# GLA cores of a hybrid encoder: split float32r products, float32r transposes and a moved query projection

## Chip, cores and metric

The kernel runs on one core of one Trainium2 chip. The metric is the device time of one execution in microseconds (us). A core has five engines with a queue each: PE (TensorE, matrix products and transposes; its weight loads are shown apart as PEld), DVE (VectorE), ACT (ScalarE), POOL (GpSimd) and SP, which here only issues DMAs. ACT and POOL issue DMAs too.

## What is computed

A two-layer encoder over 512 tokens of width 1024. Layer 0 mixes tokens by bidirectional gated linear attention (GLA), layer 1 by softmax attention; each is followed by a gated MLP with a width-3 convolution. The change lies in the GLA mixer alone, which in the reference is, cut to its core:

```python
GLA_HEADS, GLA_DK, GLA_DV, GLA_CHUNK = 4, 128, 256, 64
proj = h @ w_in                        # q, k, v, g, r
la_f = heads(log_sigmoid(r_f @ w_up_f + b_f) / 16)     # and la_b, backward

def gla_chunked(q, k, v, log_a, strict):
    b = cumsum(log_a, axis=3)          # within a chunk
    b_end = b[:, :, :, -1:, :]
    q_dec, k_inv = q * exp(b), k * exp(-b)
    att = where(mask, einsum('bhncd,bhnsd->bhncs', q_dec, k_inv), 0.0)
    o_intra = einsum('bhncs,bhnsv->bhncv', att, v)
    kv_chunk = einsum('bhncd,bhncv->bhndv', k * exp(b_end - b), v)
    # s_prev: scan over chunks, state = decay_chunk * state + kv_chunk
    o_inter = einsum('bhncd,bhndv->bhncv', q_dec, s_prev)
    return (o_intra + o_inter).reshape(B, H, S, dv)

o_f = gla_chunked(q, k, v, la_f, strict=False)
o_b = flip(gla_chunked(flip(q), flip(k), flip(v), flip(la_b), strict=True))
o = rmsnorm(o_f + o_b, norm_w) * silu(g)
return o @ w_out
```

## The kernel before

Activations lie transposed, features on partitions and tokens along the free dimension: `x` is eight tiles of 128 x 512. Most products are done in "split float32r": an operand is written as a high part, rounded to float32r by a copy on ACT, and a low part, the difference, by a subtraction on DVE. A product is then three float32r products, high x high, high x low and low x high (`mm3`, L347 to L351). Weights come by SP's DMAs in raw form and are split on ACT and DVE (`split`, L198 and L199) one or two pieces ahead of use, in three buffers.

The program is written as straight code; a planner then decides, with its own estimate of each operation's time, in which order each engine takes its instructions, the earlier one in the program first among those that it thinks ready. The estimate fixes the order only: on the chip each engine waits for what its next instruction needs. Tiles come from tagged pools with a fixed number of buffers; the PSUM banks are "acc" (3), "s" (2), "pt" (2) and "po" (1), and the SBUF tags of concern are "t" (6), "u" (4), "g" (22, made by `big`), "xhl" (8) and "ring" (1). `tc.issue_after(ins)` ties instructions behind another one on the same engine.

The GLA (`gla`, from L426) first projects values `v` and gates `g` for all heads, with the decays of all heads and both directions beside them (`gate`: `EK[h, d]` holds the two exponentials, 512 columns for queries and 512 for keys, `FK[h, d]` the decays of super-chunks of 128 tokens). Then come the four heads. Each has

- `proj(h)`: 24 products for the keys (psk) and 24 for the queries (psq), each multiplied by the token norm on DVE (L550, L553) into `kqt`. Head h+1 is projected in the program before head h's core.
- `core(h)`: for each direction DVE multiplies the key exponential by the keys and the query exponential by the queries, in place (L561, L562), and POOL makes the keys weighted to the end of the super-chunk (`ends`, L565). PE transposes these in float32 (kt, L572), ACT copies them out (kts, L574). PE makes inner products of keys and queries in float32 (in, L584); ACT copies the forward ones (`at`, L586), DVE puts the backward ones over them above the diagonal (L589). PE makes keys times v in float32 (kv, L607), ACT and DVE sum these to the states (L608, L610), in PE's order three for each direction; the third goes to bank "po". Then the last head's tail, then the outputs (L631): for each of four groups of 128 tokens `at` times v and up to two products with states, all float32. Squares on ACT (L635), a reciprocal root on POOL (L283), and the scaling by the gates on DVE into `g` (L638).
- `tail(h)`: PE transposes the gated outputs in float32 (tp, L644), ACT and DVE split them (L646, L647) into a tile of tag "xhl" each for the out-projection.

Beside head 0, ACT takes the gates' silu and POOL multiplies them by the norm weights (L653). After head 3, twelve steps of the out-projection (op, L406) run before head 3's tail.

Of the kernel before, what the change touches and what calls it, by code (L numbers as in the profile page):

```python
# [20 lines left out]
GH, DK, DV = 4, 128, 256  # L21
# [33 lines left out]
def hybrid_encoder_kernel(  # L55
# [30 lines left out]
    def nm(s):  # L86
        uid[0] += 1
        return f"{s}{uid[0]}"
# [15 lines left out]
    def tiny(w, n, tag="tiny"):  # L104
        return sp.tile([P, 8], F32, tag=tag, bufs={"tiny": 36, "tiny2": 4}[tag], name=nm(n))[:, :w]
# [141 lines left out]
    for c in range(KC):  # L247
        r = slice((c % 4) * S, (c % 4 + 1) * S)
# [26 lines left out]
    def rsqrt_eps(src, w, n, scale=None, tag="tiny"):  # L275

        t = tiny(w, n, tag)
        if scale is None:
            dve.tensor_scalar(t, src, EPS, None, ALU.add)
        else:  # L280
            dve.tensor_scalar(t, src, scale, EPS, ALU.mult, ALU.add)
        r = tiny(w, n, tag)
        pool.tensor_tensor(r, t, halfneg[:, :w], ALU.pow)  # L283
        return r
# [62 lines left out]
    def mm3(ps, wh, wl, mh, ml, start, stop):  # L347

        mm(ps, wh, mh, start=start, stop=False)  # L349
        mm(ps, wh, ml, start=False, stop=False)  # L350
        mm(ps, wl, mh, start=False, stop=stop)  # L351

    def feature_steps(wh, wl, hl, ps):

# [71 lines left out]
    def gla(norm, nxt):  # L426
# [115 lines left out]

        oh = [None] * KC

        def proj(h):
            kqt = big(F32, "kq")
            tag = "acc" if h else "pt"
            psk = bank(tag, "k")
            feature_tile(*W.half(w_kq, 2 * h), norm.hl, psk)
            dve.tensor_tensor(kqt[:, S:], psk, norm.R, ALU.mult)  # L550
            psq = bank(tag, "q")
            feature_tile(*W.half(w_kq, 2 * h + 1), norm.hl, psq)
            dve.scalar_tensor_tensor(kqt[:, :S], psq, DK ** -0.5, norm.R, ALU.mult, ALU.mult)  # L553
            return kqt

        def core(h, kqt, then):
            ends = big(F32, "end")
            ends = [ends[:, :S], ends[:, S:]]
            for d in range(2):
                e, f = EK[h, d], ends[d]  # L560
                dve.tensor_tensor(e[:, S:], e[:, S:], kqt[:, S:], ALU.mult)  # L561
                dve.tensor_tensor(e[:, :S], e[:, :S], kqt[:, :S], ALU.mult)  # L562
                sup = slice(0, 3) if d == 0 else slice(1, 4)
                v3 = lambda t: t.rearrange("p (s t) -> p s t", t=P)[:, sup, :]
                pool.tensor_tensor(v3(f), v3(e[:, S:]), FK[h, d][:, sup].rearrange("p (s o) -> p s o", o=1)  # L565
                                   .to_broadcast([P, 3, P]), ALU.mult)

            orders, keys = ([0, 1, 2], [3, 2, 1]), []
            for d, order in enumerate(orders):
                kt = bank("pt", "kt")  # L570
                for i, s in enumerate(order):
                    pe.transpose(kt[:, i * P : (i + 1) * P], ends[d][:, s * P : (s + 1) * P], ident)  # L572
                kts = tmp("t", "kts")
                act.activation(kts[:, : 3 * P], kt[:, : 3 * P], AF.Copy)  # L574
                keys.append(kts)

            at = tmp("t", "at")
            banks = []
            for d in range(2):
                e = EK[h, d]  # L580
                b = bank("acc" if h == GH - 1 else "s", "in")
                for s in range(NT):
                    o = s * P
                    mm(b[:, o : o + P], e[:, S + o : S + o + P], e[:, o : o + P], start=True, stop=True)  # L584
                banks.append(b)
            act.activation(at, banks[0], AF.Copy)  # L586

            def upper():
                dve.copy_predicated(at3, msk, banks[1].rearrange("p (s c) -> p s c", c=P))  # L589

            at3 = at.rearrange("p (s c) -> p s c", c=P)
            msk = smask.rearrange("p (o c) -> p o c", o=1).to_broadcast([P, NT, P])

            st = {}
            hs = slice(h * DV, (h + 1) * DV)
            for d, order in enumerate(orders):
                kts = keys[d]
                sa = tmp("t", "sa")
                sb = tmp("t", "sb") if d == 0 else st["b"]
                st["b"] = sb  # L600
                step = 1 if d == 0 else -1
                kv = bank("acc", "kv")
                kv2 = bank("po", "kv2")
                place = [kv[:, :DV], kv[:, DV:], kv2[:, :DV]]
                slot = [sa[:, :DV], sa[:, DV:], sb[:, d * DV : (d + 1) * DV]]
                for i, s in enumerate(order):
                    mm(place[i], kts[:, i * P : (i + 1) * P], v[s][:, hs], start=True, stop=True)  # L607
                act.activation(slot[0], place[0], AF.Copy)  # L608
                for i in (1, 2):
                    last = dve.scalar_tensor_tensor(slot[i], slot[i - 1], FK[h, d][:, order[i] : order[i] + 1],  # L610
                                                    place[i], ALU.mult, ALU.add)
                for i, s in enumerate(order):
                    st[d, s + step] = slot[i]
                if d == 0:
                    with tc.issue_after(last.ins) if h == GH - 1 else ExitStack():
                        upper()
            if then is not None:
                then()

            oss = tiny(4, "oss")  # L620
            og = []
            for s in range(NT):
                if s % 2 == 0:
                    bo = bank("s", "o")
                po = bo[:, (s % 2) * DV : (s % 2 + 1) * DV]
                parts = [(at[:, s * P : (s + 1) * P], v[s][:, hs])]
                for d in range(2):
                    if (d, s) in st:
                        parts.append((EK[h, d][:, s * P : (s + 1) * P], st[d, s]))
                for i, (l, r) in enumerate(parts):  # L630
                    mm(po, l, r, start=i == 0, stop=i == len(parts) - 1)  # L631
                og.append(po)
            for s in range(NT):
                junk = tmp("sq", "junk", DV)
                act.activation(junk, og[s], AF.Square, accum_out=oss[:, s : s + 1])  # L635
            ors = rsqrt_eps(oss, NT, "ors", 1.0 / DV)
            for s in range(NT):
                dve.scalar_tensor_tensor(g[s][:, hs], og[s], ors[:, s : s + 1], g[s][:, hs], ALU.mult, ALU.mult)  # L638

        def tail(h):  # L640
            for c in (2 * h, 2 * h + 1):
                tp = bank("pt", "tp")
                for s in range(NT):
                    pe.transpose(tp[:, s * P : (s + 1) * P], g[s][:, c * P : (c + 1) * P], ident)  # L644
# [3 lines left out]
                oh[c] = (t[:, :S], t[:, S:])  # L648

        kqt = proj(0)  # L650
        for j in range(NT):
            act.activation(g[j], g[j], AF.Silu)
            pool.tensor_tensor(g[j].rearrange("p (h c) -> p h c", c=DV), g[j].rearrange("p (h c) -> p h c", c=DV),  # L653
                               gnw.rearrange("p (o c) -> p o c", o=1).to_broadcast([P, GH, DV]), ALU.mult)
# [495 lines left out]
```

## Time and profile before

| | us |
|---|---|
| median of three runs | 1116.74 |
| the three runs | 1116.59, 1116.74, 1118.1 |
| the profiled execution | 1117.63 |
| its span, first to last instruction | 1115.9 |
| PE busy in it | 1110.2 |
| DVE, ACT, POOL busy | 792.9, 550.3, 120.6 |

The granted clock of PE was 1.0 in the whole execution. Times within the profile count from the span's start; a row of a timeline has the start, the length, the engine, the line of the kernel, the operation, the tile written, the tiles read, the shape and how many instructions are merged, and in brackets how long the engine had been idle and what released it. Matrix products overlap in PE's pipeline, so that the length of one (0.39 us for 512 columns) is more than the distance to the next; the chain of waits gives the distances.

### The profile page before, as it was taken

The page shows a single profiled execution, that of the slowest core. Times are in us where ns is not written, and L with a number is a line of the kernel's source. Part 1 is how long each engine was busy: PE and PEld are TensorE (multiplying, and loading weights), DVE is VectorE, ACT ScalarE, POOL GpSimd, SP SyncE. Part 2 cuts the span into 40 slices and gives each one's busy share as a digit, 9 for nine tenths or more (in the row PEclk, how much of TensorE's full clock was granted, in tenths as well). Part 3 has the DMA queues.
Part 4 walks back from the last instruction along what each step waited for, and adds up shares of the span by engine and source line. Part 5 has one row for each costly group of instructions (what it writes and reads, how often), then busy time and mean ns, then how long its engine had stood idle before and what let it go on. Part 6 is the DMA issues. An engine that isn't in the chain of part 4 may idle for free.

```text
span 1115.9 us, 14785 instructions
## 1 busy us (share of the span) xinstructions
PE 1110.2 (99%) x5836; PEld 953.7 (85%) x5836; DVE 792.9 (71%) x1221; ACT 550.3 (49%) x818; POOL 120.6 (11%) x114
## 2 busy tenths in 40 slices
PE   9999999999999999999999999999999999999998
PEld 7888888888889988898888888888888998889887
DVE  6786654577789677975755688756778957797572
ACT  5565233444556444553464667644454644465340
POOL 0104110000101000100004343000010100010000
PEclk9999999999999999999999999999999999999999
DMA  6322220223226523363247765422222652336322
GB/s 234 144 83 76 76 76 25 90 78 111 76 76 171 156 90 113 95 157 125 97 118 186 192 174 161 140 88 85 104 76 76 171 165 80 113 95 170 115 76 76
DMA packets 30790, 128.57 MB, mean 115 GB/s; under 512 B 3584, under 2 KB 4224, under 8 KB 20352
## 3 DMA queue, kind: packets, MB, share of 16 engines
q1 hardware_dynamic: 21216, 102.30, 26.8%
q0 software_dynamic: 4608, 16.78, 7.9%
q10 hardware_dynamic: 4896, 8.54, 2.0%
q8 instruction: 46, 0.75, 0.3%
q14 instruction: 24, 0.20, 0.1%
HBM read 100.34 MB, written 2.10 MB: 92 GB/s over the span
## 4 chain that ended last, share of the span: by engine, by line
PE 98%; DVE 1%; DMA 0%; issue 0%; ACT 0%; ACTq 0%; SPq 0%; DVEq 0%
PE r L754 14%; PE up L349 14%; PE up L350 14%; PE up L351 14%; PE op L406 8%; PE vg L380 8%; PE dn L351 2%; PE dn L350 2%; PE dn L349 2%; PE o L631 2%; PE av L380 1%; PE kv L607 1%; PE A L349 1%; PE A L350 1%; PE A L351 1%; PE pt L1009 1%
## 5 line engine op out<-in xcount | busy, mean ns | idle before, releaser
L349 PE MATMUL up<-xhl,wh 128*128 128x512 f32 x704 | 274.4, 390 | 0.0
L350 PE MATMUL up<-xhl,wh 128*128 128x512 f32 x704 | 274.0, 389 | 0.0
L351 PE MATMUL up<-xhl,wl 128*128 128x512 f32 x704 | 273.9, 389 | 0.0
L198 ACT ACTIVATE wh<-raw 128x1024 fp32r<-128x1024 f32 x132 | 139.5, 1057 | 227.3 <-PE up L350 108.4
L199 DVE TENSOR_TENSOR wl<-raw,wh 128x1024 fp32r<-128x1024 f32 x132 | 164.3, 1245 | 40.2 <-ACT wh L198 40.0
L351 PEld LDWEIGHTS up<-xhl,wl 128*128 128x128 f32 x704 | 132.1, 188 | 27.8
L349 PEld LDWEIGHTS up<-xhl,wh 128*128 128x128 f32 x704 | 132.2, 188 | 27.0
L350 PEld LDWEIGHTS up<-xhl,wh 128*128 128x128 f32 x704 | 132.2, 188 | 27.0
L754 PE MATMUL r<-gu,wh 128*128 128x256 f32 x640 | 116.3, 282 | 0.0
L754 PEld LDWEIGHTS r<-gu,wh 128*128 128x128 f32 x640 | 99.7, 191 | 0.3
L696 DVE TENSOR_TENSOR u<-up,R 128x512 f32<-128x512 f32 x88 | 60.1, 685 | 54.4 <-PE up L351 54.4
L754 PE MATMUL r<-gu,wl 128*128 128x256 f32 x320 | 90.4, 283 | 0.0
L698 ACT ACTIVATE y<-u,cw 128x512 f32<-128x512 f32 x88 | 71.2, 811 | 33.0 <-DVE u L696 32.8
L380 PE MATMUL vg<-wh,xhl 128*128 128x512 f32 x256 | 80.1, 391 | 0.4 <-DVE wh L196 0.4
L406 PE MATMUL op<-oT,wh 128*128 128x512 f32 x256 | 71.8, 394 | 0.0
L700 DVE SCALAR_TENSOR_TENSOR y<-u,cw,y 128x511 f32<-128x511 f32 x88 | 65.7, 748 | 2.0
L699 DVE SCALAR_TENSOR_TENSOR y<-u,cw,y 128x511 f32<-128x511 f32 x88 | 65.4, 744 | 1.2 <-ACT y L698 1.2
L702 ACT ACTIVATE y<-y 128x512 f32<-128x512 f32 x44 | 27.8, 632 | 72.0 <-DVE y L700 71.8
L754 PEld LDWEIGHTS r<-gu,wl 128*128 128x128 f32 x320 | 61.1, 191 | 0.0
L188 POOL DMA_DIRECT2D wl<-raw x32 | 28.3, 884 | 292.7 <-ACT wl L141 140.8
L380 PEld LDWEIGHTS vg<-wh,xhl 128*128 128x128 f32 x256 | 48.1, 189 | 10.9 <-ACT sq L323 0.6
L406 PEld LDWEIGHTS op<-oT,wh 128*128 128x128 f32 x256 | 47.2, 188 | 9.5 <-ACT oT L646 0.3
(221 smaller groups left out, 1936.4 us busy)
## 6 DMA issues: line engine op xcount, KB each, us to landing
raw<-in_w_up_dram SPq DMA_DIRECT2D x42, 1024.0 KB, 4.8
raw<-in_w_down_dram SPq DMA_DIRECT2D x22, 1024.0 KB, 4.8
wl<-raw POOLq DMA_DIRECT2D x32, 512.0 KB, 4.6
ring<-p ACTq DMA_DIRECT2D x26, 256.0 KB, 2.7
raw<-in_w_vg_dram SPq DMA_DIRECT2D x6, 1024.0 KB, 4.9
raw<-in_w_kq_dram SPq DMA_DIRECT2D x4, 1024.0 KB, 4.8
raw<-in_w_gout_dram SPq DMA_DIRECT2D x4, 1024.0 KB, 4.8
raw<-in_w_aout_dram SPq DMA_DIRECT2D x16, 256.0 KB, 4.1
```

The costliest lines, as they stand in the source:

```text
L198: act.activation(hi[:, sl], r[:, sl], AF.Copy)
L199: dve.tensor_tensor(lo[:, sl], r[:, sl], hi[:, sl].bitcast(F32), ALU.subtract)
L349: mm(ps, wh, mh, start=start, stop=False)
L350: mm(ps, wh, ml, start=False, stop=False)
L351: mm(ps, wl, mh, start=False, stop=stop)
L380: mm(ps[j][:, :width], hl[k][i == 2][:, j * P : (j + 1) * P], (wl if i == 1 else wh)[:, sl], start=k == 0 and i == 0, stop=k == KC - 1 and ...
L406: mm(pss[ng][n], wt[:, sl], mv, start=k == 0 and i == 0, stop=k == KC - 1 and i == 2)
L696: dve.tensor_tensor(u, ps, norm.R, ALU.mult)
L698: act.activation(y, u, AF.Identity, scale=w(1), bias=w(3))
L699: dve.scalar_tensor_tensor(y[:, 1:], u[:, : S - 1], w(0), y[:, 1:], ALU.mult, ALU.add)
L700: dve.scalar_tensor_tensor(y[:, : S - 1], u[:, 1:], w(2), y[:, : S - 1], ALU.mult, ALU.add)
L754: mm(dst, w[:, sl], m, start=start and j == 0 and a == 0, stop=j == NQ - 1 and a == 2, skip_group_check=True)
```

## The change

- Keys times v and `at` times v are done in split float32r, three products each. The transposed keys (`kth`, `ktl`), the inner products (`ath`, `atl`) and the head's v (`values(h)`, one tile "ring") are split for it on ACT and DVE. Products with states and inner products remain in float32.
- Transposes of keys and of gated outputs read float32r copies, which DMAs on ACT's queue make of `ends` (two for each head) and of `g` (four for each head).
- The keys weighted to the end are made on DVE instead of POOL.
- `core` is cut in parts. Order in the program: kproj(0), keys(0), gates, qproj(0), and then for each head inner(h), kproj(h+1), keys(h+1), values(h), outer(h), qproj(h+1). Within `outer` all `at` products stand first, then the last head's tail, then the products with states from the last token group to the first, each tied behind the one before it on PE; qproj(h+1) is tied behind the last of them.
- The second direction's third key-value product goes to a bank of "acc" instead of "po"; the last head's inner products go to "s" like the others'; split outputs of heads 0 and 1 lie in tiles of "g", not "xhl".

```diff
-        def proj(h):
+        def kproj(h):
...
             dve.tensor_tensor(kqt[:, S:], psk, norm.R, ALU.mult)
+            return kqt
+
+        def qproj(h, kqt):
+            psq = bank("acc" if h else "pt", "q")
             feature_tile(*W.half(w_kq, 2 * h + 1), norm.hl, psq)
...
+        def keys(h, kqt):
+            ends, copies = big(F32, "end"), big(F32R, "endr")
             for d in range(2):
...
                 dve.tensor_tensor(e[:, S:], e[:, S:], kqt[:, S:], ALU.mult)
-                dve.tensor_tensor(e[:, :S], e[:, :S], kqt[:, :S], ALU.mult)
...
-                pool.tensor_tensor(v3(f), v3(e[:, S:]), FK[h, d][:, sup].rearrange("p (s o) -> p s o", o=1)
+                dve.tensor_tensor(v3(f), v3(e[:, S:]), FK[h, d][:, sup].rearrange("p (s o) -> p s o", o=1)
...
+                act.dma_start(r[:, cols].bitcast(F32), f[:, cols])
+            return copies
...
+        def inner(h, kqt, copies):
             for d in range(2):
                 e = EK[h, d]
-                b = bank("acc" if h == GH - 1 else "s", "in")
+                dve.tensor_tensor(e[:, :S], e[:, :S], kqt[:, :S], ALU.mult)
+                b = bank("s", "in")
                 for s in range(NT):
...
+            for d, order in enumerate(ORDERS):
+                kt = bank("pt", "kt")
+                for i, s in enumerate(order):
+                    pe.transpose(kt[:, i * P : (i + 1) * P].bitcast(F32R),
+                                 copies[:, d * S + s * P : d * S + (s + 1) * P], identr)
+                hi, lo = f32r("t", "kth")[:, : 3 * P], f32r("u", "ktl")[:, : 3 * P]
+                act.activation(hi, kt[:, : 3 * P], AF.Copy)
+                dve.tensor_tensor(lo, kt[:, : 3 * P], hi.bitcast(F32), ALU.subtract)
...
+            hi, lo = f32r("u", "ath"), f32r("u", "atl")
+            act.activation(hi, at, AF.Copy)
+            dve.tensor_tensor(lo, at, hi.bitcast(F32), ALU.subtract)
...
+        def values(h):
+            t = sp.tile([P, 4 * S], F32R, tag="ring", bufs=1, name=nm("vr"))
+            for s in range(NT):
...
+                act.activation(hi, r, AF.Copy)
+                dve.tensor_tensor(t[:, 2 * S + s * DV : 2 * S + (s + 1) * DV], r, hi.bitcast(F32), ALU.subtract)
...
+        def outer(h, rows, at, vs):
...
-                kv2 = bank("po", "kv2")
+                kv2 = bank("acc" if d else "po", "kv2")
...
-                    mm(place[i], kts[:, i * P : (i + 1) * P], v[s][:, hs], start=True, stop=True)
+                    last = mm3(place[i], kh[:, sl], kl[:, sl], *vs[s], True, True)
...
+                for i, (l, r) in enumerate(((at[0], vs[s][0]), (at[0], vs[s][1]), (at[1], vs[s][0]))):
+                    mm(og[s], l[:, sl], r, start=s % 2 == 0 and i == 0, stop=False, skip_group_check=True)
+            if h:
+                last = tail(h - 1)
+            for s in reversed(range(NT)):
+                parts = [(EK[h, d][:, s * P : (s + 1) * P], st[d, s]) for d in range(2) if (d, s) in st]
                 for i, (l, r) in enumerate(parts):
-                    mm(po, l, r, start=i == 0, stop=i == len(parts) - 1)
+                    with tc.issue_after(last.ins):
+                        last = mm(og[s], l, r, start=False, stop=i == len(parts) - 1, skip_group_check=True)
...
+            gr[h] = big(F32R, "gr")
             for s in range(NT):
                 dve.scalar_tensor_tensor(g[s][:, hs], og[s], ors[:, s : s + 1], g[s][:, hs], ALU.mult, ALU.mult)
+                act.dma_start(gr[h][:, s * DV : (s + 1) * DV].bitcast(F32), g[s][:, hs])
...
         def tail(h):
-            for c in (2 * h, 2 * h + 1):
+            t3 = gr.pop(h)
+            for c in range(2):
                 tp = bank("pt", "tp")
                 for s in range(NT):
-                    pe.transpose(tp[:, s * P : (s + 1) * P], g[s][:, c * P : (c + 1) * P], ident)
-                t = pair("xhl", 8, F32R, "oT")
+                    last = pe.transpose(tp[:, s * P : (s + 1) * P].bitcast(F32R),
+                                        t3[:, s * DV + c * P : s * DV + (c + 1) * P], identr)
+                t = big(F32R, "oT") if h < 2 else pair("xhl", 8, F32R, "oT")
...
-        kqt = proj(0)
+        kqt = kproj(0)
+        copies = keys(0, kqt)
         for j in range(NT):
             act.activation(g[j], g[j], AF.Silu)
...
+        qproj(0, kqt)
         for h in range(GH):
-            nxtk = proj(h + 1) if h + 1 < GH else None
-            core(h, kqt, (lambda: tail(h - 1)) if h else None)
-            kqt = nxtk
+            rows, at = inner(h, kqt, copies)
+            if h + 1 < GH:
+                kqt = kproj(h + 1)
+                copies = keys(h + 1, kqt)
+            vs = values(h)
+            last = outer(h, rows, at, vs)
+            if h + 1 < GH:
+                with tc.issue_after(last.ins):
+                    qproj(h + 1, kqt)
```

More of the change, by code (lines that the diff above doesn't have):

```diff
@@ L350, in mm3 @@
         mm(ps, wh, ml, start=False, stop=False)
-        mm(ps, wl, mh, start=False, stop=stop)
+        return mm(ps, wl, mh, start=False, stop=stop)
     def feature_steps(wh, wl, hl, ps):
@@ L553, in proj, with f32r @@
             dve.scalar_tensor_tensor(kqt[:, :S], psq, DK ** -0.5, norm.R, ALU.mult, ALU.mult)
[L554 to L558, printed above, removed]
+        ORDERS = ([0, 1, 2], [3, 2, 1])
+        def f32r(tag, n):
+            return sp.tile([P, S], F32R, tag=tag, bufs={"u": 4, "t": 6}[tag], name=nm(n))
+        def keys(h, kqt):
+            ends, copies = big(F32, "end"), big(F32R, "endr")
             for d in range(2):
-                e, f = EK[h, d], ends[d]
+                e = EK[h, d]
+                f, r = ends[:, d * S : (d + 1) * S], copies[:, d * S : (d + 1) * S]
@@ L569, in core @@
[L569 to L577, printed above, removed]
+                dve.tensor_tensor(v3(f), v3(e[:, S:]), FK[h, d][:, sup].rearrange("p (s o) -> p s o", o=1)
+                                  .to_broadcast([P, 3, P]), ALU.mult)
@@ L606, in core @@
                 for i, s in enumerate(order):
-                    mm(place[i], kts[:, i * P : (i + 1) * P], v[s][:, hs], start=True, stop=True)
+                    sl = slice(i * P, (i + 1) * P)
+                    last = mm3(place[i], kh[:, sl], kl[:, sl], *vs[s], True, True)
                 act.activation(slot[0], place[0], AF.Copy)
                 for i in (1, 2):
-                    last = dve.scalar_tensor_tensor(slot[i], slot[i - 1], FK[h, d][:, order[i] : order[i] + 1],
-                                                    place[i], ALU.mult, ALU.add)
+                    dve.scalar_tensor_tensor(slot[i], slot[i - 1], FK[h, d][:, order[i] : order[i] + 1],
+                                             place[i], ALU.mult, ALU.add)
                 for i, s in enumerate(order):
                     st[d, s + step] = slot[i]
[L614 to L620, printed above, removed]
             og = []
```

35 lines of the change are left out of this document (19 added, 16 removed).

## The prediction

> **What bounds the kernel now.** I read first the page's totals and the chain of work that ended last.
>
> ```profile
> span 1115.9 us, 14785 instructions
> PE 1110.2 (99%) x5836; PEld 953.7 (85%) x5836; DVE 792.9 (71%) x1221; ACT 550.3 (49%) x818; POOL 120.6 (11%) x114
> PE 98%; DVE 1%; DMA 0%; issue 0%; ACT 0%; ACTq 0%; SPq 0%; DVEq 0%
> ```
>
> TensorE (PE) is busy 1110.2 of 1115.9 us and is 98% of the chain: the kernel is as long as PE's own list of work, and 5.7 us of the whole span are gaps. So a change can win only by making PE's list shorter, and loses whatever gaps it opens. Next I read the chain in order of time for one head of the GLA (head 2), and in it the pieces that the change touches.
>
> ```profile
> 163.52 0.23 PE q L351
> 163.75 0.66 PE kt L572 x6
> 164.41 1.79 PE in L584 x16
> 166.20 2.16 PE kv L607 x10
> 168.36 0.33 PE tp L644 x3
> 168.69 0.65 PE kv L607 x2
> 169.34 0.55 PE tp L644 x5
> 169.88 4.32 PE o L631 x20
> ```
>
> Columns are start, length, what. A head's core takes 10.45 us of PE without a pause (163.75 to 174.20): transposes of the keys, inner products, keys times v, transposes of the last head's outputs, outputs. A float32 product is two PE instructions here. Note that the eight tp are split around the last two kv. In the program all tp stand behind all kv: the order on an engine is planned, ready work being put where the planner expects a wait. That matters below.
>
> Then the groups by line and shape from 90 to 220 us, for the counts over four heads, and for the only stall:
>
> ```profile
> L607 PE MATMUL kv<-v,kts 128*128 128x256 f32 x48 | 12.1, 388 | 0.0
> L631 PE MATMUL o<-v,at 128*128 128x256 f32 x32 | 9.4, 379 | 0.0
> L572 PE MATMUL kt<-ident,end 128*128 128x128 f32 x24 | 3.3, 272 | 0.0
> L644 PE MATMUL tp<-ident,g 128*128 128x128 f32 x32 | 4.6, 272 | 0.0
> PEld kv L607 <- DVE sb L610: 0.9, 4, 0.3
> ```
>
> **What PE saves.** A 256-column float32 product costs 2 x 2.16/10 = 0.432 us. What the new forms cost is shown by other stages: the down-projection's split float32r products of 256 columns, and attention's float32r transposes.
>
> ```profile
> 341.16 38.69 PE r L754 x324
> 640.64 0.29 PE pt L1009 x4
> ```
>
> One float32r product of 256 columns takes 38.69/324 = 0.119 us, three of them 0.358. That is 0.074 us less for each of 24 kv and 16 at-times-v products (48 and 32 instructions above): 2.95 us. A float32 transpose takes 0.66/6 = 0.11 us, a float32r one 0.29/4 = 0.073: 0.0375 us for each of 56 (24 kt, 32 tp), 2.1 us. The 0.9 us of kv waiting for bank "po" goes too, since the second direction's third product now takes an "acc" bank. What is late next there is treated below. Sum: 5.95 us less. Inner products and the products with states stay in float32 and are not touched.
>
> **What the other engines get.** For each head: two end-of-chunk products move from POOL to VectorE (DVE); DVE gains these, two subtractions of 384, one of 512 and four of 256; ACT gains one copy of 512, four of 256, and six DMA issues (two key copies, four gr).
>
> ```profile
> L608 ACT ACTIVATE sa<-kv 128x256 f32<-128x256 f32 x8 | 3.1, 384 | 8.3 <-PE kv L607 8.3
> L586 ACT ACTIVATE at<-in 128x512 f32<-128x512 f32 x4 | 2.4, 599 | 0.0
> L610 DVE SCALAR_TENSOR_TENSOR sb<-sa,fk,kv 128x256 f32<-128x256 f32 x8 | 3.8, 480 | 0.8
> 117.31 0.69 DVE L561 TENSOR_TENSOR ek<-ek,kq 128x512 f32<-128x512 f32 x1
> L997 ACTq DMA_DIRECT2D ring<-p x26: 472/472/1072, 625.8 to 720.5; - x26
> DMA to landing us min/median/max: 2.2/2.5/6.5
> 131.47:142.38 10.91, 10.91 (x50) 8.96 (x50) 4.95 (x9) 2.10 (x6) 2.60 (x3) 1.00 0.18 50
> 142.38:152.82 10.44, 10.44 (x63) 9.33 (x62) 5.61 (x9) 3.79 (x10) 0.00 (x0) 1.00 0.12 49
> ```
>
> The last two rows are one head's period (21.35 us; columns stretch, length, PE, PEld, DVE, ACT, POOL): DVE works 10.6 us of it, ACT 5.9. A 384-wide DVE operation I put at 0.58 (between 0.48 at 256 and 0.69 at 512). DVE gains 4 x 0.58 + 0.69 + 4 x 0.48 = 4.9 us, ACT 0.60 + 4 x 0.38 + 6 x 0.47 = 4.9. Both stay under 16 of some 20 us, so neither becomes the bound as an average. What costs is order. The copies of v depend only on v and on the one "ring" tile, free when the last head's at-products are done, one whole query projection (5.45 us) earlier: nothing. The ACT queue's DMAs stand behind the DVE result they copy, and behind them wait the next casts and key copies. The 2.5 us to landing are hidden in heads 1 to 3, where keys and gr are made a projection before they are used. For the last head's outputs the cover is the out-projection:
>
> ```profile
> 186.97 1.66 DVE L638 SCALAR_TENSOR_TENSOR g<-o,ors,g 128x256 f32<-128x256 f32 x4 [1.12 <-POOL ors L283]
> 184.71 16.37 PE op L406 x72
> ```
>
> g is ready at 188.63, four issues and a landing make 193.0, and the transposes are due at 201.1: nothing. The eight queries' and keys' projections cost the same in any order.
>
> **Head 0: the wait that the new order opens.** Before, a head's keys and queries were both ready one whole projection pair ahead. Now q(0) is the last thing before head 0's inner products, and only k(1), 24 products, can stand between. The rows of that stretch:
>
> ```profile
> 101.36 2.35 DVE L199 TENSOR_TENSOR wl<-raw,wh 128x1024 fp32r<-128x1024 f32 x1 [0.34 <-ACT wh L198]
> 105.70 0.69 DVE L550 TENSOR_TENSOR kq<-k,R 128x512 f32<-128x512 f32 x1 [2.00 <-PE k L351]
> 106.43 2.44 DVE L561 TENSOR_TENSOR ek<-ek,kq 128x512 f32<-128x512 f32 x1
> 108.27 2.84 POOL L653 TENSOR_TENSOR g<-g,gconst 128x1024 f32<-128x1024 f32 x1
> 108.79 3.42 DVE L199 TENSOR_TENSOR wl<-raw,wh 128x1024 fp32r<-128x1024 f32 x1
> 110.94 0.39 PE L349 MATMUL k<-xhl,wh 128*128 128x512 f32 x1
> 112.12 1.31 DVE L561 TENSOR_TENSOR ek<-ek,kq 128x512 f32<-128x512 f32 x1
> 113.36 0.68 DVE L553 SCALAR_TENSOR_TENSOR kq<-q,R 128x512 f32<-128x512 f32 x1
> 117.92 1.22 DVE L199 TENSOR_TENSOR wl<-raw,wh 128x1024 fp32r<-128x1024 f32 x1
> ```
>
> While POOL multiplies the gates (four operations to 108.27 + 2.84 = 111.11), a DVE operation with two SBUF inputs takes 2.44 instead of 0.69 us, or 3.42 instead of 1.22: the one issued at 108.79 ends at 112.21, as if it had begun when POOL stopped. L550, which reads PSUM, is not touched. The Trainium skill ("SBUF — State Buffer", section "Who interferes with whom") has it that a VectorE instruction with two SBUF inputs and a GpSimd one that reads SBUF exclude each other for a whole instruction; the rows agree.
>
> After the change DVE has, from 106.43: ek (to 108.87), then the moved product, blocked to 111.11 and done at 111.7, ek and product of the other direction (113.0), a weight split (114.2), kq of q (114.9), ek of q (115.6). The first key copy lands about 111.7 + 2.5 = 114.2. PE ends q(0) at 110.94. Does the plan know? The order of before answers: at 112.12 DVE runs ek of direction 1 although q, which stands earlier in the program, has been finished since about 111.2. The planner thus expected DVE to be far ahead, without POOL's hindrance: keys done by about 109, copies landed near 111. So it will put kt first and "in" some 1.5 us later, and PE stands until 114.2: about 3.3 us. Ends: 0, if the plan places 16 or more of k(1)'s products ahead, and 115.6 - 110.94 = 4.7 with none. Were there no exclusion, the product would be done near 109.4 and this term would be about 0.4, the sum near -3.6 us. I take 3.3.
>
> **The other gaps.** The chain from q to "in" in a quiet stretch:
>
> ```profile
> 163.36 0.39 PE L351 MATMUL q<-xhl,wl 128*128 128x512 f32 x1
> 163.79 0.69 DVE L553 SCALAR_TENSOR_TENSOR kq<-q,R 128x512 f32<-128x512 f32 x1 [1.03 <-PE q L351]
> 164.52 0.69 DVE L562 TENSOR_TENSOR ek<-ek,kq 128x512 f32<-128x512 f32 x1
> ```
>
> PE is free at 163.59 and "in" could start near 165.3, 1.7 us later. In heads 1 and 2 the kt (0.44) and k(h+1) fill it, in the last head kt and, if banks allow, products of the out-projection. Where before filled such a wait with tp it fell short by 0.9/4 = 0.22 us; three times that is 0.7. If the out-projection isn't drawn forward, the last head loses 1.3; I take 0.3, as ready work was drawn forward before. Second, DVE takes the next head's keys (0.69 x 3 + 0.58 x 2 = 3.2 us), which stand earlier in the program, ahead of the state sums: these end about 0.2 + 3.2 + 2 x 0.58 = 4.55 us behind k(h+1). PE needs 18 x 0.119 + 12 x 0.119 = 3.6 us for kv and at-products, and 0.58 for tails from head 1 on. That leaves 1.0 in head 0 and 0.4 in heads 1 and 2, where nothing else may be drawn forward, as q is tied behind the outputs. Ends 0 and 1.8; I take 1.0.
>
> Sum: -5.95 + 3.3 + 0.7 + 0.3 + 1.0 = -0.65 us. The profiled execution took 1117.63 (span 1115.9 and 1.7 around it), so it would take 1117.0; the median of three is 0.89 lower, 1116.74, which gives 1116.1. About 0.2%, 2.2 us, is what can be told from no change.
>
> **Rivals.** *Head 0 is covered* (chance 0.30): the planner lays most of k(1) ahead of kt and "in". Then the term 3.3 falls away: -3.95 us, 1112.8; with every gap at 0, 1110.8. For it speaks that 5.45 us of ready products stand there; against it the DVE order at 112.12.
>
> *Too little filler in every head* (0.19), the slower end: the plan sets "in" directly behind kt. PE then stands 4.7 in head 0, 1.3 in each of the other three, 1.8 at the state sums, and 0.6 in the last head, where at, its masking and its split (some 3 us) outlast kv and tp. 11 us against 5.95: +5.05, 1121.8. It decides from gaps of 6 us on, that is from about one and a half microseconds a head. Against it: tp were drawn between kv. The Trainium skill ("TensorE: Matmul & The Clock Gate", section "Why this matters for your kernels") warns that PE gaps over about 3 us halve the clock; no row here has such a gap, and by it a gap of head 0's size could cost some 1.7 us more, an estimate from the 3.4 us at half rate that the page gives.
>
> *The split saves nothing* (0.04): a product waits for its weights' load. At the mean of all loads, 953.7/5836 = 0.163 us, three would cost 0.49 instead of 0.432: the 40 products lose 2.3 instead of gaining 2.95, and the sum would be +4.6, 1121.3. The spacing of 0.119 in 324 such products in a row speaks against it.
>
> **How the numbers follow.** The forecast has 0.47, of which 0.08 lies under 1114.5 and 0.06 over 1119.0. Faster: 0.08 + 0.28 = 0.36; slower: 0.06 + 0.17 + 0.04 = 0.27; the rest, 0.37, within 0.2%. The range goes from 1112.0, which holds the covered case, to 1120.5, about half way into the slower one.
>
> **What would show it.** In the profile after: kv in 72 instructions 0.12 us apart, at-products in 48, transposes 0.073 apart; PE idle about 3 us between 111 and 116, put down to a key copy or DVE; DVE's moved product lasting over 2 us in head 0 and 0.6 later; small PE waits for sb at the outputs of heads 0 to 2. I am wrong if PE has no gap near 111, or if gaps over 1 us stand behind q in heads 1 to 3.

## The result and the profile after

| | before | after |
|---|---|---|
| median of four runs, us | 1116.76 (1116.59 to 1118.1) | 1124.29 (1123.02 to 1125.55) |
| profiled execution | 1117.63 | 1123.02 |
| its span | 1115.9 | 1121.3 |
| first key product of head 0 | 100.06 | 102.18 |
| from it to the first product of the MLP | 129.25 | 132.86 |

After is slower: ratio 1.0065, 95% interval 1.0047 to 1.0082. The prediction said 1116.1 within 1112.0 to 1120.5; it was wrong. The last two rows are starts of PE's rows in the two timelines. They place the loss of 5.4 us in the span: 2.1 before the heads begin, in code that the change does not touch, and 3.6 in the heads; the rest of the kernel gives 0.3 back.

The page of after, its totals and the chain of work:

```profile
span 1121.3 us, 14944 instructions
...
PE 1107.1 (99%) x5876; PEld 952.4 (85%) x5876; DVE 806.8 (72%) x1257; ACT 555.7 (50%) x838; POOL 113.9 (10%) x106
...
PE 90%; DVE 3%; DMA 1%; ACT 1%; issue 1%; POOL 0%; ACTq 0%; DVEq 0%
```

PE has 3.1 us less to do (1110.2 before) and stands 14.2 us instead of 5.7. It was 98% of the chain and is 90%: the other engines have come into it. What PE's loads waited for, in the whole of after (line, releaser, us, times, longest):

```profile
PEld kt L593 <- DVE ek L583: 3.6, 1, 3.6
PEld o L660 <- DVE sb L640: 1.8, 2, 0.9
PEld kv L349 <- ACT kth L596: 1.6, 1, 1.6
PEld kt L593 <- DMA endr<-end: 1.4, 1, 1.4
...
PEld z L500 <- issue: 1.2, 1, 1.2
PEld z L500 <- DVE gm L505: 1.1, 2, 0.7
...
PEld in L587 <- DVE ek L583: 0.4, 2, 0.3
```

None of these seven stood in before's list, whose one wait in the heads' cores was 0.9. Five lie in the heads, 8.8 us; the two of z (the products that give the decays) lie in the decay stage. The first is put down to DVE; the copy of the keys ended last there, as PE's timeline says (below). The spacing of the products came out as costed (PE's timeline, head 1):

```profile
145.26 0.28 PE L349 MATMUL kv<-vr,kth 128*128 128x256 f32 x1
145.38 0.28 PE L350 MATMUL kv<-vr,kth 128*128 128x256 f32 x1
145.50 0.28 PE L351 MATMUL kv<-vr,ktl 128*128 128x256 f32 x1
...
148.85 0.79 PE L676 MATMUL tp<-ident,gr 128*128 128x128 f32 x8
150.39 0.70 PE L660 MATMUL o<-sb,ek 128*128 128x256 f32 x2 [0.75 <-DVE sb L640]
```

kv products start 0.12 apart, eight transposes take 0.79 with the pipeline's end, and behind them PE stands 0.75 for a state. The new waits of 8.8 less the old 0.9 would make the stage 7.9 us longer, and it grew by 3.6. The remainder, 4.3, is put down to the shorter products, where 5.05 was predicted. PE's busy time between the two starts of the table, read directly, fell by 3.7 (129.22 to 125.55), so the saving lies between 3.7 and 4.3.

**The decay stage.** The timelines of DVE, ACT and POOL:

```profile
35.05 2.02 DVE L616 TENSOR_TENSOR vr<-v,vr 128x256 fp32r<-128x256 f32 x1
36.99 0.68 DVE L486 TENSOR_TENSOR rf<-rp,R 128x512 f32<-128x512 f32 x1
...
31.98 0.42 ACT L615 ACTIVATE vr<-v 128x256 fp32r<-128x256 f32 x1 [0.24 <-DVE v L449]
32.30 1.04 ACT L477 ACTIVATE gst<-graw 128x1024 fp32r<-128x1024 f32 x1
...
33.48 3.30 POOL L478 TENSOR_TENSOR gst<-graw,gst 32x1024 fp32r<-32x1024 f32 x1 [2.66 <-ACT gst L477]
```

The chain of work goes on with the load of the next weights:

```profile
36.81 4.72 DMA raw<-in_w_vg_dram
```

The copies of head 0's v depend on v alone, and the planner drew them some 70 us forward, between the steps of the decays (tied behind the silu, in the first experiment, ACT takes the first of them at 103.34). ACT took two of them (the row at 31.98 is the second) ahead of gst, the rounded weights of the decays, which started at 29.09 before and starts at 32.30. POOL's remainder of it moved from 30.75 to 33.48, and SP's next weight load, which stands behind it, from 33.15 to 36.81. On DVE the first remainder of v (2.02; the others take 0.36 each) ends when POOL's operation ends, at 36.8 to 37.1, and rf, the input of the decays' products z, which started at 35.00 before, comes after it. PE then waits at z.

**Head 0.** The timelines of DVE and POOL:

```profile
108.74 2.77 DVE L199 TENSOR_TENSOR wl<-raw,wh 128x1024 fp32r<-128x1024 f32 x1
111.44 3.48 DVE L569 TENSOR_TENSOR ek<-ek,kq 128x512 f32<-128x512 f32 x2
114.84 1.01 DVE L572 TENSOR_TENSOR end<-ek,fk 128x384 f32<-128x384 f32 x2
...
102.32 11.45 POOL L688 TENSOR_TENSOR g<-g,gconst 128x1024 f32<-128x1024 f32 x4 [65.53 <-issue]
```

And the chain:

```profile
115.42 2.20 DMA endr<-end
...
117.75 0.42 PE kt L593 x3
```

While POOL multiplies the gates, to 113.77, a weight split takes 2.77 instead of 1.22 us and the two key products 3.48 (1.29 for those of head 2 at 146.19, below); the copy is issued at 115.42 and has landed at 117.6. PE had taken six products of k(1) and stands from 114.58 to 117.75.

**Heads 1 and 2, and the last head.** DVE around the state sums of head 1, then ACT before the last head's kv:

```profile
146.19 1.29 DVE L569 TENSOR_TENSOR ek<-ek,kq 128x512 f32<-128x512 f32 x2
147.40 1.02 DVE L572 TENSOR_TENSOR end<-ek,fk 128x384 f32<-128x384 f32 x2
...
148.72 1.22 DVE L199 TENSOR_TENSOR wl<-raw,wh 128x1024 fp32r<-128x1024 f32 x1
149.86 0.47 DVE L640 SCALAR_TENSOR_TENSOR sb<-sa,fk,kv 128x256 f32<-128x256 f32 x1
...
177.91 2.43 ACTq L668 DMA_DIRECT2D gr<-g  x4
180.39 1.06 ACT L198 ACTIVATE wh<-raw 128x1024 fp32r<-128x1024 f32 x1 [4.32 <-DMA gr<-g]
181.35 0.85 ACT L596 ACTIVATE kth<-kt 128x384 fp32r<-128x384 f32 x2
```

The state sum sb stands behind the next head's keys, as predicted, and also behind a weight split. In the last head ACT holds back a cast and the keys' rounding until it has issued four copies of gated outputs, each of which must first be made.

### The profile page after: what moved, and what is told of

It is laid out like the page before. It is cut to its first block, busy times and chain, and to the rows that moved or that the text cites. A ratio compares the mean times of both kernels' runs of the same rounds, so it can differ in the third digit from the quotient of the medians.

```text
span 1121.3 us, 14944 instructions
## 1 busy us (share of the span) xinstructions
PE 1107.1 (99%) x5876; PEld 952.4 (85%) x5876; DVE 806.8 (72%) x1257; ACT 555.7 (50%) x838; POOL 113.9 (10%) x106
## 4 chain that ended last, share of the span: by engine, by line
PE 90%; DVE 3%; DMA 1%; ACT 1%; issue 1%; POOL 0%; ACTq 0%; DVEq 0%
PE r L796 14%; PE up L350 14%; PE up L349 14%; PE up L351 14%; PE op L406 8%; PE vg L380 4%; PE dn L350 2%; PE dn L349 2%; PE dn L351 2%; PE av L380 1%; PE o L660 1%; PE A L349 1%; PE A L350 1%; PE A L351 1%; PE B L349 1%; PE B L351 1%
```

## The experiments

Nine kernels were run. Each is told by its median, with its ratio to runs of before on the same chip, and by the stage of the table above (first key product to the MLP's first product, in the profiled execution):

| kernel | median, us | ratio to before | stage starts | stage |
|---|---|---|---|---|
| before | 1116.76 | | 100.06 | 129.25 |
| after | 1124.29 | 1.0065 | 102.18 | 132.86 |
| v's copies late | 1122.57 | 1.0055 (1.0040 to 1.0070) | 99.63 | 134.40 |
| no gate product | 1121.15 | 1.0037 (1.0024 to 1.0051) | 101.77 | 130.91 |
| state sums first | 1125.96 | 1.0075 (1.0056 to 1.0094) | 104.08 | 135.07 |
| order alone | 1121.14 | 1.0036 (1.0023 to 1.0049) | 99.94 | 134.36 |
| split in the old order | 1118.46 | 1.0014 (1.0005 to 1.0024) | 99.27 | 130.66 |
| keys ahead of head 0 | 1120.73 | 1.0038 (1.0023 to 1.0053) | 102.08 | 130.06 |
| mended | 1117.05 | 1.0001 (0.9988 to 1.0013) | 100.08 | 128.24 |
| mended, copies by GpSimd | 1115.30 | 0.9990 (0.9981 to 0.9998) | 99.69 | 127.17 |
| mended, float32 | 1117.73 | 1.0004 (0.9996 to 1.0013) | 99.76 | 129.84 |

**v's copies late.** Head 0's copies of v are tied behind the last silu, past the decay stage.

```diff
-            vs = values(h)
+            with tc.issue_after(silu.ins) if h == 0 else ExitStack():
+                vs = values(h)
```

> The split of head 0's v is tied behind the gates' silu on ACT, so that it can't be drawn into the decay stage at 31 to 38 us, where its copies stand before the cast of the decay weights. Theory A (the planner draws ready low-priority work in front of due work and opens waits): the 2.1 us by which PE already trails before's times when head 0's keys start goes away, about 1122.2 us, and the waits in the cores stay. Rival B (the lag before the cores has another cause, such as the clock or code loading): no change, 1124.3, and PE still waits at z.

The waits at z are gone and the heads start at 99.63: 2.5 us earlier than in after. Of these, 0.6 lie ahead of the copies' place already (DVE starts on v at 29.94, in after at 30.53), which leaves some 2.0 for the copies. The median fell by 1.7, as Theory A had it within 0.4. The whole 2.5 did not arrive in the profiled execution, because of something new behind head 0's gap. A window of this kernel (stretch, length, busy times of PE, PEld, DVE, ACT and POOL, granted clock, DMA):

```profile
115.00:118.00 3.00, 2.78 (x12) 2.62 (x13) 3.00 (x5) 0.73 (x2) 0.00 (x0) 0.54 0.09 32
```

And PE's row of head 0's inner products:

```profile
116.59 2.93 PE L587 MATMUL in<-ek 128*128 128x128 f32 x16
```

After a gap of 3.2 us at kt the granted clock is 0.54 in the mean of three microseconds, and sixteen inner products take 2.93 (1.95 elsewhere). In after's own profiled execution the same gap was followed by a clock of 1.00.

**No gate product.** POOL's multiplication of the gates by the norm weights (L688) is left out, so that DVE is not held in head 0.

```diff
-            pool.tensor_tensor(g[j]..., g[j]..., gnw..., ALU.mult)
```

> POOL's product of the gates and the norm weights is left out (the output is then not the reference's); PE's order is that of the changed kernel. Theory A (in head 0 PE waits for key copies that are late because DVE's products with two SBUF inputs are held up while POOL works): the 3.2 us wait at kt falls under 0.5 and DVE's products of head 0 take 0.6 to 0.7 us each; about 1121.1 us. Rival B (the wait is that of the copy's landing and of DVE's own list): at least 2 us of the wait stay, 1123.5 or more.

Theory A has the time right (1121.15), but the wait fell by 2.0, not below 0.5. The list of the loads' waits, DVE's timeline and the chain of work:

```profile
PEld kt L593 <- DVE ek L583: 1.6, 1, 1.6
...
108.33 1.23 DVE L199 TENSOR_TENSOR wl<-raw,wh 128x1024 fp32r<-128x1024 f32 x1 [0.23 <-ACT wh L198]
109.48 1.29 DVE L569 TENSOR_TENSOR ek<-ek,kq 128x512 f32<-128x512 f32 x2
...
111.27 3.94 DMA endr<-end
```

DVE is free, as Theory A had it: the weight split takes 1.23 us (2.77 in after) and the two key products 1.29 (3.48). The first key copy is issued 9.5 us behind head 0's first key product; in after it was 13.2. So POOL's hold is worth 3.7 us, as much as the whole wait. The 1.6 us that stay come from the copy: it took 3.94 us to land, after's 2.20, as in rival B. It ran beside a weight load that was issued at 109.6 (the DMA engines' share was 0.73 to 1.00 from 111 to 115); that the load delayed it is inferred. Had it landed in 2.20, an estimate, it would have been there at 113.5, before PE had ended its six products of filler at 114.2.

The profiled execution fell by 1.9, the median by 3.1; the rest fits the granted clock, 0.999 or 1.0 in all five of its runs.

**State sums first.** The next head's keys stand behind the head's outputs in the program.

```diff
                 kqt = kproj(h + 1)
-                copies = keys(h + 1, kqt)
...
             last = outer(h, rows, at, vs)
+                copies = keys(h + 1, kqt)
```

> The next head's key products are put behind this head's outputs in the program, so that DVE takes the state sums first. Theory A: the two waits of outputs for state sums (0.75 each) and the 1.2 us wait of head 0's outputs behind the next head's key transposes go; in heads 1 to 3 the key transposes follow the inner products, filled by k; about 1.5 to 2.5 us less, 1122.2. Rival B (DVE is simply full, so that the wait moves to the key copies): 1124 or more with waits at kt in heads 1 to 3.

Theory A missed: the waits for sb are gone, but the time did not fall, since the waits for the keys grew:

```profile
PEld kt L593 <- DVE ek L583: 6.8, 2, 3.6
```

The keys now come too late for the copy by DMA in the last head too, and a second gap of about 3 us opens there. Both gaps were followed by half clock (the sixteen inner products take 3.59 and 3.03 us). In this order the wait moves from the state sums to the keys; rival B held. That the kernel is slower than after itself is not shown: the intervals of the two ratios overlap, and the 1.9 us by which its heads start later were lost before DVE starts on v (32.46, in after 30.53), in code that this edit does not touch.

**Order alone.** Everything in float32 as before, `ends` on POOL, no copies: only the new order of projections, outputs and banks.

```diff
-                    last = mm3(place[i], kh[:, sl], kl[:, sl], *vs[s], True, True)
+                    last = mm(place[i], kts[:, sl], v[s][:, hs], start=True, stop=True)
...
-                                 copies[...], identr)
+                    pe.transpose(kt[...], copies[...], ident)
...
-            vs = values(h)
+            vs = None
```

> The new program order alone: all products and transposes in float32 as before, end products on POOL, no copies, no split of v. Theory A (the order opens the waits, the split is a gain): slower than before by the waits of head 0 (about 3) and some of those at the state sums (0 to 1.5), without the loss in the decay stage: 1119 to 1121 us. Rival B (the split and its copies bring all of the loss, the order none): 1117 us.

It costs 4.4 us with nothing split, as Theory A had it within 0.2; the whole change costs 7.5. The two are not shares of one sum, since the split also saves. PE stands 2.4 us at head 0's kt (for POOL's end product, which queues behind the gates), and the clock falls again. PE's timeline and two windows:

```profile
113.40 0.78 PE L591 MATMUL kt<-ident,end 128*128 128x128 f32 x3 [2.42 <-POOL end L572]
```

```profile
114.00:115.00 1.00, 1.00 (x4) 0.81 (x4) 1.00 (x1) 0.49 (x1) 0.67 (x1) 0.50 0.00 0
115.00:116.00 1.00, 1.00 (x6) 0.80 (x5) 1.00 (x2) 0.00 (x0) 0.00 (x0) 0.50 0.00 0
```

**Split in the old order.** The other half: split, float32r transposes and copies as in after, but a head's keys and queries projected together ahead of the last head's core, and v's copies late.

```diff
+            now = kqt, copies
+            if h + 1 < GH:
+                kqt = kproj(h + 1)
+                copies = keys(h + 1, kqt)
+                qproj(h + 1, kqt)
-            rows, at = inner(h, kqt, copies)
+            rows, at = inner(h, *now)
```

> The split products, float32r transposes and copies with the projections in the order of before (keys and queries of the next head ahead of a head's core, queries not tied); head 0's v split behind the silu. Theory A (the order opens the waits, the split itself shortens PE's list by about 5 us): faster than before, 1112 to 1115 us, with no wait over 1 us in head 0. Rival B (the split's longer chain from inner products to at, and the copies, stop PE wherever they stand): 1118 us or more.

Theory A missed by over 3 us. The rounding and the remainder hang a longer chain between kt and kv. Most of the wait for it lies in the last head (1.7 of 2.7), where nothing ready stands there:

```profile
PEld kv L349 <- ACT kth L596: 2.7, 3, 1.7
...
PEld in L587 <- DVE g L667: 0.8, 1, 0.8
PEld o L652 <- DVE atl L606: 0.7, 2, 0.5
```

```profile
176.15 3.43 PE L587 MATMUL in<-ek 128*128 128x128 f32 x16 [0.61 <-DVE g L667]
```

These are 4.2 us of waits, and the last row shows the inner products of the last head at half clock, 3.43 instead of 1.95; the whole stretch at half clock cost 1.7. Less the old wait of 0.9 and the 3.7 that PE's list is shorter, that makes 1.3, and the stage grew by 1.4. So the split needs the filler that the new order was to give, and the new order needs other work in head 0; neither half gains alone.

**Keys ahead of head 0.** After, with 21 of the 24 products of k(1) ahead of head 0's inner products in the program.

```diff
+        nxk = kproj(1)
+        for _ in range(7):
+            next(nxk)
         for h in range(GH):
```

> Of head 1's key projection, 21 of 24 products are put ahead of head 0's inner products, nothing else is changed. Theory A (head 0 stands for want of work that may pass): its 3.6 us wait falls under 0.5, and with it the half clock behind it, so 1124.3 falls by 3.5 to 5.5 to about 1119.8, the runs lie closer together and the granted clock is 1.0. Rival B (the wait follows DVE and only moves): less than 1.5 us gained.

Head 0's wait is gone, and the median falls by 3.6, to within 1 us of what was expected. The waits for sb grow from 1.8 to 3.3, since head 0 now has one too, so that 1.5 of the 3.6 come back there. This is the rival "head 0 is covered" of the prediction, made by hand: its mechanism was right, only the planner did not do it.

**Mended.** v's copies late, keys ahead of head 0, the next head's keys between the state sums and the at products, inner products tied behind the last output product.

```diff
+            mid()                      # keys(h + 1), behind the state sums
             og = []
...
-            rows, at = inner(h, kqt, copies)
+            with tc.issue_after(last.ins) if h else ExitStack():
+                rows, at = inner(h, kqt, copies)
```

> The changed kernel with the waits that its trace shows mended: head 0's v split behind the silu, 21 products of k(1) ahead of head 0's inner products, the next head's key products between the state sums and the at-products in the program, the next head's transposes tied behind this head's outputs. Theory A: of 11 us of waits about 2.5 stay (key copies of the last head 1.6, inner products 0.4, the rest small), so the list's 5.95 us comes through as 3 to 4: 1112.5 to 1114 us, faster than before. Rival B (DVE and ACT are too full in order, and mended waits come back elsewhere): 1116 or more.

It equals before and missed the expectation by some 3 us. The profiled execution took 1116.24, 6.8 less than after's; two kinds of wait are left in the heads that cost over a microsecond each in total.

```profile
PEld kv L349 <- ACT kth L604: 2.0, 1, 2.0
...
PEld in L595 <- DVE ek L591: 1.2, 2, 0.9
```

Four of its ten runs have a mean granted clock of 0.998; their median is 1118.8, that of the other six 1116.2.

**Mended, copies by GpSimd.** One line more: the copies of heads 0 to 2 are issued by POOL.

```diff
-                act.dma_start(gr[h][...].bitcast(F32), g[s][:, hs])
+                (act if h == 3 else pool).dma_start(gr[h][...].bitcast(F32), g[s][:, hs])
```

> The mended kernel once more, with one edit: the copies gr of the gated outputs of heads 0 to 2 are issued by GpSimd's queue instead of ScalarE's. In the mended kernel's trace ScalarE stood in those four issues (170.85 2.78 ACTq L677 x4, waiting for g) and then in a weight's cast (173.67 1.06) before the last head's keys' rounding (174.63 kth), and TensorE waited 2.0 us for it. Theory A (the wait is ScalarE's queue held by the copies' issues): the wait kv <- kth is gone and the time falls by about 2, to 1114.3 profiled and 1115 in the median of the runs. Rival B (the chain k, transposes, rounding, remainder is too long for the last head's short filler, whoever issues the copies): a wait of over 1 us stays, on kth or ktl, and the time stays over 1116.

1115.3, by 1.75 under the mended kernel and 0.1% under before (the interval ends at 0.9998): the one kernel here that is below both. That it is faster than the mended kernel is less certain: the two ran on different chips, and the intervals of their ratios to before overlap. Of the 1.9 us between their profiled executions 1.1 lies in the stage; the rest lies in code that the edit does not touch. ACT's and PE's timelines in the last head:

```profile
172.16 1.06 ACT L198 ACTIVATE wh<-raw 128x1024 fp32r<-128x1024 f32 x1 [3.66 <-PE q L350]
173.12 0.85 ACT L604 ACTIVATE kth<-kt 128x384 fp32r<-128x384 f32 x2
...
173.64 0.38 PE L349 MATMUL kv<-vr,kth 128*128 128x256 f32 x1 [0.84 <-ACT kth L604]
```

The queue's hold is gone; what is left of the wait (0.84 in PE's row, 1.0 in the list of the loads' waits, where the mended kernel has 2.0) is the weight cast, which the plan put ahead of kth, and kth itself. Theory A has the time right and the wait only halved; that the time came out is in part luck. None of its twelve runs has a clock under 0.999, where four of ten had in the mended kernel. That would fit a gap of 2 us bringing the clock down in some runs, but no trace of such a run is there to show it.

**Mended, float32.** The mended order with float32 products and transposes and no copies.

```diff
-                    last = mm3(place[i], kh[:, sl], kl[:, sl], *vs[s], True, True)
+                    last = mm(place[i], kts[:, sl], v[s][:, hs], start=True, stop=True)
...
-                                 copies[...], identr)
+                    pe.transpose(kt[...], copies[...], ident)
...
-            gr[h] = big(F32R, "gr")
```

> The mended order (key projections ahead of head 0's inner products, next keys behind the state sums, inner products tied behind the last output products) with the arithmetic of before: kv and the at products in float32, no copies of v, transposes of the float32 tiles, no copies for them. Theory A (the split and the copied transposes save what the prediction's list says, 2.95 + 2.1 = 5.05 of TensorE's time, and the rest of the change is order): TensorE's busy time rises by about 5 over the mended split kernel's, and with the waits on kth, z and ek away (about 3) the time is about 1119. Rival B (most of the split's gain is eaten by the longer chains that it hangs in front of TensorE): it is within 1 of the mended split kernel's 1117, at 1116 to 1118.

The totals of this kernel and its window from the first key product to the MLP, then both of the mended kernel with copies by GpSimd:

```profile
PE 1109.6 (99%) x5836; PEld 953.9 (86%) x5836; DVE 793.7 (71%) x1229; ACT 548.9 (49%) x818; POOL 113.0 (10%) x106
...
99.76:229.60 129.84, 129.19 (x633) 109.19 (x632) 76.25 (x116) 45.88 (x93) 15.49 (x8) 1.00 0.19 67
```

```profile
PE 1105.1 (99%) x5876; PEld 951.9 (86%) x5876; DVE 804.7 (72%) x1257; ACT 556.2 (50%) x838; POOL 119.8 (11%) x118
...
99.69:226.86 127.17, 125.50 (x673) 107.41 (x672) 87.29 (x144) 52.99 (x113) 22.34 (x20) 1.00 0.28 97
```

PE's busy time differs by 4.5 us in the whole kernel, but by 3.7 in the stage (129.19 to 125.50); the other 0.8 lies in code that is the same in both. So the split and the transposes take about 3.7 from PE's list, where 5.05 was predicted. At 1117.73 the float32 kernel lies 0.7 above the mended split kernel, as rival B expected, and 2.4 above the one with the copies on POOL, whose stage is 2.7 shorter: about two thirds of the saving arrive in the time even then. The mended order alone costs 1 us against before or nothing (the interval includes 1). What the change gains is thus brought by the split and the float32r transposes together, which no run separates, and the order must first be made free.

## Why the prediction was wrong, step by step

- **PE's list.** 5.05 of shorter products predicted; 4.3 as the remainder of the waits and 3.7 by PE's busy time measured. The 0.9 at "po" went as said. Right in kind, 0.8 to 1.3 too large.
- **Head 0's wait**, 3.3: measured 3.6, with POOL's hold on DVE, the copy's landing and a plan that seems to have known nothing of either. The mechanism was right. The rule quoted there from the Trainium skill ("SBUF — State Buffer", section "Who interferes with whom") agrees with the rows at 108.74 and 35.05, and without POOL's product the same weight split took 1.23 us. But the size came out partly by luck. The copy landed 4.6 us behind the first product of k(1) (113.06 to 117.62), not 3.3, and six products of k(1), 1.4 us, which the prediction did not put there, made up for it. POOL held a weight split and the key products; the moved product, which the prediction wanted to see blocked for over 2 us, was not held (1.01 for both).
- **The shortfall at "in"**, 0.7: measured 0.4.
- **The state sums**, 1.0 with an end of 1.8: 1.8, the end, but in heads 1 and 2, which had been given 0.4 each; a weight split stands ahead of the sums there as well. Too small by 0.8. And head 1's kt waited 1.4 for its copy, because the planner drew it between head 0's output products. I had treated copies as hidden in heads 1 to 3, at nothing. Together this failed by 2.2.
- **The last head**, 0.3 with an end of 1.3: 1.6. I counted the four issues as work of ACT (0.47 each) and noted what queues behind them, but put no price on it. Failed by 1.3. In the mended kernel, where this wait was 2.0, moving the issues to POOL halved it, so the queue was about half of it there and the weight cast ahead of the keys' rounding the rest. It stands behind q as a gap of 1.47 us in PE's row, which the prediction had named as a sign of being wrong.
- **The copies of v, costed at nothing.** Failed by 2.1 (2.0 in the run that ties them back), the largest single term. I named what they depend on and concluded that they cannot be late. I did not ask whether they can be early: the same prediction says that the planner draws ready work forward.

In sum -5.2 (4.3 and the 0.9) + 3.6 + 0.4 + 3.2 + 1.6 + 2.1 = +5.7 for the heads and the decay stage, and 0.3 given back elsewhere make the 5.4 of the two profiled executions. This closes by construction, since the 4.3 is the remainder of the same waits. The terms that were too small are of one kind: work that is ready sooner, or held later, than I had costed it.

The step to the median failed apart from that, by 2.2. I took 0.89 off the profiled time, as before's median lies below it. After's lies 1.27 above: 1123.02 had a mean clock of 0.999, the other runs, 1123.78 to 1125.55, 0.998 to 0.997. One stretch of 3.4 us at half clock takes 1.7 us and 0.0015 off the mean, so those runs fit one or two such stretches. Their stretches were not seen, since only the profiled executions have a trace. Runs of before reached 1119.5 at a clock of 0.999 or 1.0, so the clock need not be all of it.

Of the rivals, "too little filler in every head" gave 1121.8 and came nearest: a wait in every head, 8.8 us of its 11. But its price in head 0 was too high and it had no place for the decay stage. I held it at 0.19 because tp had been drawn between kv; in after they stood in one block of eight behind the `at` products in heads 1 and 2 (148.85 and 170.07) and filled none of these waits. "The split saves nothing" is refuted by the spacing of 0.12.

## What to carry to other kernels

Of work that becomes ready long before its use, ask in which earlier stage a planner will put it and tie it down there: "off the path" holds only for the place that one thought of. Price each DMA issue by what stands behind it on its queue while it waits for its data, not by its own length. When an edit shortens the bounding engine's list, count the filler left at each of its dependent chains: of some 4 us saved here about 2.5 came through even in the best kernel.

## What the runs showed of the hardware

- The granted clock fell to 0.50 behind some gaps of PE: 2.42 us (order alone), 3.19 (v's copies late), 3.17 and 2.88 (state sums first), and 1.58 and 0.61 within 2.5 us (split in the old order; its window 175 to 180 has a mean clock of 0.66). It did not fall behind 3.17 us in after, nor behind 1.85 in the mended kernel. In order alone the three windows of 2 us from 112 have a clock of 0.89, 0.50 and 0.75, which is 1.7 us of full clock missing, or about 3.4 us at half. The Trainium skill ("TensorE: Matmul & The Clock Gate", section "Why this matters for your kernels") advises against gaps over about 3 us; the gaps of order alone and of split in the old order were shorter, so the safe gap here is smaller, and whether a gap is hit differs between executions. The same page (section "What's actually happening") has the window in which activity is watched run free of the kernel, which would fit that difference between executions; no run here shows the window itself. The prediction's estimate of 1.7 us for one such stretch agrees with the windows.
- Copies issued by POOL landed as soon as those by ACT (2.2 and 2.1 us in the median of the DMA view), and PE's waits show none that the move added.
